# Moving a transposed activation tile by 128 bytes within SBUF in a two-layer float32 trunk

## The chip, the cores and the metric

The kernel runs on one core of a Trainium2 chip. The metric is the device time of one execution in microseconds (us), lower is better; the number given for a kernel is the median of several executions. One further execution of the kernel before was recorded by the hardware profiler, and all rows below come from that one.

## The reference

The input is one sequence of 256 tokens with 1024 channels in float32. Two layers follow each other, and each is a macaron: a feed-forward block, a token mixer, a second feed-forward block, each with an RMS norm before and after.

```python
def swiglu_ffn(x, w_in, w_out):
    gate, up = jnp.split(x @ w_in, 2, axis=-1)
    return (jax.nn.silu(gate) * up) @ w_out

for layer in range(DEPTH):
    g = norm_gains[layer]
    h = swiglu_ffn(rms_norm(x, g[0]), ffn_w_in[layer, 0], ffn_w_out[layer, 0])
    x = x + 0.5 * rms_norm(h, g[1])
    hn = rms_norm(x, g[2])
    # even layer: causal Conformer convolution; odd layer: HGRN2 gated recurrence
    x = x + rms_norm(m, g[3])
    h = swiglu_ffn(rms_norm(x, g[4]), ffn_w_in[layer, 1], ffn_w_out[layer, 1])
    x = x + 0.5 * rms_norm(h, g[5])
```

The hidden width of a feed-forward block (FFN) is 2816. Nearly all the arithmetic is matrix products of the activations with weights that are read from HBM once.

## The kernel before

**Precision.** Every float32 operand is split in two float32r tiles, a rounded high part and the remainder, and a product is made of three matmuls: high by high, high by low, low by high. `weight` (L121) fetches half a megabyte of weights into a `raw` tile (four buffers) and `split` (L135) makes `wh` on ScalarE (L136) and `wl` on VectorE (L137), ten buffers each.

**The transposed input.** `xt` (L101) holds the current activations transposed, channels on the partitions, as eight channel blocks `k` of 2048 bytes per partition: 256 columns of the high part, then 256 of the low part. `pre_norm` (L168) and the convolution's `turn` (L540) refill it ahead of each block. It is used in two ways:

- as the moving operand, with a weight block loaded into TensorE: `channels` (L324) in the FFNs. For each of two parts (PSUM tiles `mm` and `tr`) it runs eight matmuls of 512 columns on `wh` (L331) and then eight of 256 columns on `wl` (L333). `channel_pair` (L341) does the like with 256 columns throughout (L350 to L352), in the HGRN2 mixer;
- as the loaded (stationary) operand, with weights moving, 512 columns each: `project` (L291, L292, L295), and `mm3` (L140 to L142) from `boot` and from the convolution's output product.

The FFN's second product, `down` (L420), and the HGRN2 mixer's output product go through the same `mm3`, lines and weight tiles, but load other tiles: `b4` buffers (`b` in the profile) or `hid`.

An FFN loops over eleven chunks `c` of 256 hidden channels. For every chunk but the first it runs `up_both` twice (two calls of `channels`, b = 0 and 1, each with a part on `mm` and a part on `tr`), and then `down` for both halves of the tokens, 24 matmuls of 512 columns in a row.

**Where tiles stand.** Tiles of the pool `const` are placed one behind the other in the order of the code. Two tiles that nothing reads, `before_xt` and `after_xt`, stand around `xt`; together they take 512 bytes per partition. In the built program `xt` begins at byte 26144 of each partition, 32 beyond a multiple of 512. All buffers of `raw`, `wh`, `wl`, `b4`, `hid`, `e`, `ga` begin 160 beyond one. Slices of `xt`, of the weights and of `b4` that matmuls use are multiples of 512 bytes from the beginning of their tile, so a matmul on `xt` has its two operands 128 bytes apart modulo 512, and a matmul of `down` has them at the same place.

The order of the instructions on each engine is the order of the code; weights are fetched ahead, as far as buffers are free.

Of the kernel before, what the change touches and what calls it, by code (L numbers as in the profile page):

```python
# [8 lines left out]
F32 = mybir.dt.float32  # L9
# [7 lines left out]
P = 128  # L17
# [23 lines left out]
def trunk_kernel(  # L41
# [17 lines left out]
    const = ctx.enter_context(tc.tile_pool(name="const", bufs=1))  # L59
# [37 lines left out]
    pool.memset(ones, 1.0)  # L97

    xs = [const.tile([P, D], F32, name=f"x{t}") for t in range(NT)]
    const.tile([P, 88], F32, name="before_xt")  # L100
    xt_all = const.tile([P, NT * 2 * D], F32R, name="xt")  # L101
    const.tile([P, 40], F32, name="after_xt")
    xhl = xt_all.rearrange("p (k s t m) -> p k s t m", t=NT, s=2, m=P)
    gcol = const.tile([P, G_END], F32, name="gcol")

# [837 lines left out]
```

## Time and profile before

| | us |
|---|---|
| median of three runs | 1014.41 |
| lowest, highest | 1013.71, 1016.5 |
| the profiled execution | 1014.49 |
| its span, first to last instruction | 1012.6 |
| TensorE (PE) busy in it | 997.6 |
| VectorE (DVE) busy | 750.1 |
| ScalarE (ACT) busy | 548.2 |

The profile lists every instruction with its start and its length. On TensorE a matmul's length says little: matmuls are pipelined, each row shows some 390 ns for 512 columns, and the next one starts long before that has passed. What counts is the distance from one start to the next, called the pitch below. It is read from the timeline: the difference of two start times, divided by the number of matmuls between. Times in these rows are rounded to 10 ns, so a pitch is taken over many matmuls.

### The profile page before, as it was taken

To read this page: it belongs to the slowest core of one execution; us is meant where nothing else is said; L and a number is where in the kernel's file an instruction comes from. 1 tells how busy PE (TensorE), PEld (TensorE's weight loads), DVE (VectorE), ACT (ScalarE), POOL (GpSimd) and SP (SyncE) were. 2 spreads that over 40 slices of the span, in tenths; PEclk is the share of its full clock that TensorE was granted. 3 is DMA by queue.
4 is the path that set the end of the run, shared out by engine and by line. 5 is a ranking of instruction groups with operands and counts; after the bars stand their busy time and mean duration, and the time that the engine had idled before them with its cause. 6 is when DMAs were issued, how large, how long until landed. Compare 5 with 4: busy or idle time off the path is not lost.

```text
span 1012.6 us, 14787 instructions
## 1 busy us (share of the span) xinstructions
PE 997.6 (99%) x5412; PEld 853.8 (84%) x5412; DVE 750.1 (74%) x1274; ACT 548.2 (54%) x1000; POOL 56.3 (6%) x93
## 2 busy tenths in 40 slices
PE   9999999999899999999999999999999999999997
PEld 7888888878678888888888888889998888888886
DVE  6887667899888676767776767687788586767673
ACT  7656545764486555455755555584143384555542
POOL 1000000020021000000200000030001120000000
PEclk9999999999899999999999999999999999999999
DMA  7885645642527464646465646465232555555541
GB/s 250 277 286 166 213 170 178 236 176 97 178 102 241 166 209 167 224 155 222 167 198 176 210 165 221 163 210 181 81 125 92 179 192 183 180 195 192 184 146 41
DMA packets 50952, 182.06 MB, mean 180 GB/s; under 512 B 6048, under 2 KB 6176, under 8 KB 50880
## 3 DMA queue, kind: packets, MB, share of 16 engines
q1 hardware_dynamic: 50736, 181.09, 52.7%
q8 instruction: 42, 0.69, 0.3%
q14 instruction: 30, 0.25, 0.1%
q10 hardware_dynamic: 144, 0.03, 0.0%
HBM read 180.06 MB, written 1.05 MB: 179 GB/s over the span
## 4 chain that ended last, share of the span: by engine, by line
PE 91%; ACT 2%; DVE 2%; DMA 2%; POOL 1%; issue 1%; POOLq 0%; DVEq 0%; SPq 0%; ACTq 0%
PE mm L331 15%; PE tr L331 15%; PE acc L141 9%; PE acc L142 9%; PE acc L140 9%; PE mm L333 8%; PE tr L333 7%; PE mm L295 3%; PE mm L291 3%; PE mm L292 3%; PE tr L654 2%; DMA raw<-wts 2%; PE mm L351 2%; PE mm L352 2%; PE mm L350 1%; DVE wl L137 1%
## 5 line engine op out<-in xcount | busy, mean ns | idle before, releaser
L137 DVE TENSOR_TENSOR wl<-raw,wh 128x1024 fp32r<-128x1024 f32 (+1 forms) x386 | 400.1, 1059 | 88.1 <-ACT wh L136 62.8
L136 ACT CAST wh<-raw 128x1024 fp32r<-128x1024 f32 (+1 forms) x386 | 340.5, 921 | 125.2 <-DMA raw<-wts 74.9
L331 PE MATMUL mm<-xt,wh 128*128 128x512 f32 x640 | 164.1, 397 | 0.5 <-ACT wh L136 0.5
L331 PE MATMUL tr<-xt,wh 128*128 128x512 f32 x640 | 162.1, 395 | 0.0
L331 PEld LDWEIGHTS mm<-xt,wh 128*128 128x128 f32 x640 | 116.7, 188 | 25.7 <-ACT wh L136 1.3
L140 PE MATMUL acc<-wh,b 128*128 128x512 f32 x352 | 137.6, 391 | 0.0
L142 PE MATMUL acc<-wh,b 128*128 128x512 f32 x352 | 137.3, 390 | 0.0
L141 PE MATMUL acc<-wl,b 128*128 128x512 f32 x352 | 137.3, 390 | 0.0
L331 PEld LDWEIGHTS tr<-xt,wh 128*128 128x128 f32 x640 | 114.9, 188 | 20.9
L333 PEld LDWEIGHTS mm<-xt,wl 128*128 128x128 f32 x640 | 87.4, 188 | 7.4 <-DVE wl L137 0.2
L333 PEld LDWEIGHTS tr<-xt,wl 128*128 128x128 f32 x640 | 87.0, 188 | 7.4
L333 PE MATMUL mm<-xt,wl 128*128 128x256 f32 x640 | 90.0, 282 | 0.0
L333 PE MATMUL tr<-xt,wl 128*128 128x256 f32 x640 | 88.6, 281 | 0.0
L136 ACT CAST b<-e 128x256 fp32r<-128x256 f32 x80 | 32.5, 406 | 96.5 <-DVE e L412 96.5
L336 ACT COPY e<-tr 128x256 f32<-128x256 f32 x80 | 29.4, 367 | 89.6 <-PE tr L333 89.6
L142 PEld LDWEIGHTS acc<-wh,b 128*128 128x128 f32 x352 | 66.1, 188 | 13.9
L337 DVE TENSOR_TENSOR ga<-tr,e 128x256 f32<-128x256 f32 x80 | 33.7, 421 | 59.0 <-ACT e L336 58.8
L140 PEld LDWEIGHTS acc<-wh,b 128*128 128x128 f32 x352 | 66.1, 188 | 12.4
L141 PEld LDWEIGHTS acc<-wl,b 128*128 128x128 f32 x352 | 66.1, 188 | 12.4
L291 PE MATMUL mm<-wh,xt 128*128 128x512 f32 x176 | 70.7, 402 | 0.0
L292 PE MATMUL mm<-wl,xt 128*128 128x512 f32 x176 | 69.8, 397 | 0.0
L336 ACT COPY e<-mm 128x256 f32<-128x256 f32 x80 | 29.7, 371 | 51.4 <-PE mm L333 51.2
(180 smaller groups left out, 1253.6 us busy)
## 6 DMA issues: line engine op xcount, KB each, us to landing
raw<-wts SPq DMA_DIRECT2D x328, 512.0 KB, 4.8
b<-rows SPq DMA_DIRECT2D x10, 512.0 KB, 6.9
b<-x_turned SPq DMA_DIRECT2D x4, 256.0 KB, 6.1
x<-x_in SPq DMA_DIRECT2D x2, 512.0 KB, 7.6
out_dram<-x SPq DMA_DIRECT2D x4, 256.0 KB, 2.0
b<-dft SPq DMA_DIRECT2D x1, 371.0 KB, 6.4
ca<-masks SPq DMA_DIRECT2D x1, 192.0 KB, 4.6
b<-w_dw SPq DMA_DIRECT2D x1, 128.0 KB, 6.5
```

Source lines behind the costliest of these rows:

```text
L136: act.copy(dst_h, src)
L137: dve.tensor_tensor(dst_l, src, dst_h.bitcast(F32), op=ALU.subtract)
L140: pe.matmul(o, lh, rh, start=first, stop=False)
L141: pe.matmul(o, lh, rl, start=False, stop=False)
L142: pe.matmul(o, ll, rh, start=False, stop=last)
L291: pe.matmul(o, hi[:, k], wh[:, sl], start=k == 0, stop=False)
L292: pe.matmul(o, hi[:, k], wl[:, sl], start=False, stop=False)
L295: pe.matmul(o, a, w, start=False, stop=h == 1 and n == 3)
L331: pe.matmul(pair, block(ws[k // 2][0], k), xhl[:, k], start=k == 0, stop=False)
L333: pe.matmul(pair[:, 0], block(ws[k // 2][1], k), xhl[:, k, 0], start=False, stop=k == KD - 1)
L336: act.copy(cross, o[:, SEQ:])
L337: dve.tensor_tensor(res[:, part * SEQ : (part + 1) * SEQ], o[:, :SEQ], cross, op=ALU.add)
```

## The change

Padding is moved from behind `xt` to ahead of it. The sum stays 512 bytes, so nothing else moves.

```diff
     xs = [const.tile([P, D], F32, name=f"x{t}") for t in range(NT)]
-    const.tile([P, 88], F32, name="before_xt")
+    const.tile([P, 120], F32, name="before_xt")
     xt_all = const.tile([P, NT * 2 * D], F32R, name="xt")
-    const.tile([P, 40], F32, name="after_xt")
+    const.tile([P, 8], F32, name="after_xt")
```

`xt` now begins at byte 26272, 160 beyond a multiple of 512, as the weights do. Every instruction of all five engines stays, in the same order; in the built programs `xt`'s address is the only one that differs.

## Rows read from the trace of the kernel before

**Rows 1.** The page: TensorE's busy time and its granted clock in 40 slices.

```profile
PE 997.6 (99%) x5412; PEld 853.8 (84%) x5412; DVE 750.1 (74%) x1274; ACT 548.2 (54%) x1000; POOL 56.3 (6%) x93
...
PEclk9999999999899999999999999999999999999999
```

**Rows 2.** The page: the chain that ended last, by engine.

```profile
PE 91%; ACT 2%; DVE 2%; DMA 2%; POOL 1%; issue 1%; POOLq 0%; DVEq 0%; SPq 0%; ACTq 0%
```

**Rows 3.** Waits of PE: who for whom, us in total, times, longest.

```profile
PE mm L331 <- ACT wh L136: 0.5, 1, 0.5
```

**Rows 4.** Timeline of PE in an FFN chunk: start us, length us, instruction.

```profile
94.18 2.03 PE L331 MATMUL mm<-xt,wh 128*128 128x512 f32 x8
96.05 1.12 PE L333 MATMUL mm<-xt,wl 128*128 128x256 f32 x8
97.00 2.02 PE L331 MATMUL tr<-xt,wh 128*128 128x512 f32 x8
98.86 1.10 PE L333 MATMUL tr<-xt,wl 128*128 128x256 f32 x8
99.80 0.39 PE L140 MATMUL acc<-wh,b 128*128 128x512 f32 x1
...
100.72 0.39 PE L141 MATMUL acc<-wl,b 128*128 128x512 f32 x1
...
105.03 0.39 PE L142 MATMUL acc<-wh,b 128*128 128x512 f32 x1
```

**Rows 5.** Timeline of PE, convolution's output product: first and last of 28.

```profile
288.17 0.39 PE L142 MATMUL acc<-wh,xt 128*128 128x512 f32 x1
...
294.44 0.39 PE L142 MATMUL acc<-wh,xt 128*128 128x512 f32 x1
```

**Rows 6.** Timeline of PE, HGRN2 output product: 10 from 803.18, 28 from 805.50.

```profile
803.18 0.40 PE L141 MATMUL acc<-wl,b 128*128 128x512 f32 x1
...
805.27 0.39 PE L141 MATMUL acc<-wl,b 128*128 128x512 f32 x1
805.50 0.39 PE L142 MATMUL acc<-wh,b 128*128 128x512 f32 x1
...
811.62 0.39 PE L142 MATMUL acc<-wh,b 128*128 128x512 f32 x1
```

**Rows 7.** Timeline of PE, `channel_pair`, 256 columns: first and last of 61.

```profile
681.36 0.28 PE L350 MATMUL mm<-xt,wh 128*128 128x256 f32 x1
...
688.48 0.28 PE L350 MATMUL mm<-xt,wh 128*128 128x256 f32 x1
```

**Rows 8.** Timeline of PE, `channel_pair` later: first and last of 40.

```profile
737.02 0.29 PE L350 MATMUL mm<-xt,wh 128*128 128x256 f32 x1
...
741.70 0.28 PE L350 MATMUL mm<-xt,wh 128*128 128x256 f32 x1
```

**Rows 9.** Timeline of PE, `project`: first and last of 13.

```profile
301.90 0.40 PE L291 MATMUL mm<-wh,xt 128*128 128x512 f32 x1
...
304.70 0.40 PE L291 MATMUL mm<-wh,xt 128*128 128x512 f32 x1
```

**Rows 10.** Groups by line and shape: instructions, times, busy us, mean ns.

```profile
L331 PE MATMUL mm<-xt,wh 128*128 128x512 f32 x640 | 164.1, 397 | 0.5 <-ACT wh L136 0.5
...
L333 PE MATMUL mm<-xt,wl 128*128 128x256 f32 x640 | 90.0, 282 | 0.0
...
L291 PE MATMUL mm<-wh,xt 128*128 128x512 f32 x176 | 70.7, 402 | 0.0
...
L351 PE MATMUL mm<-xt,wh 128*128 128x256 f32 x128 | 36.4, 285 | 0.0
```

**Rows 11.** Windows of all engines, then of PE: busy us, clock, DMA share, GB/s.

```profile
0.00:12.00 12.00, 10.11 (x44) 8.57 (x45) 5.40 (x11) 7.86 (x16) 0.88 (x8) 1.00 0.82 271
...
350.00:366.70 16.70, 16.70 (x90) 1.00 0.58 189
```

**Rows 12.** Timeline of all engines: TensorE's weight load held by VectorE's split.

```profile
40.92 0.30 PEld L333 LDWEIGHTS mm<-xt,wl 128*128 128x128 f32 x2 [0.21 <-DVE wl L137]
```

## The prediction

> **What bounds the kernel now.** I read the page first. TensorE is busy for 997.6 of 1012.6 us at the full granted clock [rows 1], and it makes up 91% of the chain that ended last [rows 2]. Its waits on the makers of the weights are below a microsecond [rows 3]. So the time is a sum of matmul pitches, and the question is what sets a pitch. I read that from the timeline, start to start.
>
> In an FFN chunk eight L331 matmuls of 512 columns take 96.05 - 94.18 = 1.87 us, that is 233.8 ns each, and the next eight 1.86 us. Eight L333 matmuls of 256 columns take 0.95 and 0.94 us, some 118 ns each. `down` behind them needs 105.03 - 100.72 = 4.31 us for 19 matmuls of 512 columns, 226.8 ns each [rows 4]. `down` is about 3% quicker per matmul than L331, with the same number of columns and the same clock. It differs in many ways: another line, another order, other tiles.
>
> A cleaner pair stands in the two output products. They run the same lines L140 to L142 on the same weight buffers, and only the loaded tile differs. With `xt` loaded (128 bytes off the weights modulo 512) 27 steps take 294.44 - 288.17 = 6.27 us, 232.2 ns each [rows 5]. With `b4` loaded (the same place modulo 512) 27 steps take 811.62 - 805.50 = 6.12 us, 226.7 ns each [rows 6]. So 5.5 ns per matmul go with the place, and this is the row on which I build.
>
> Two more things are in these rows. The quick pitch isn't there from the start: after an interruption `b4`'s stream first runs 9 steps in 2.09 us, 232.2 ns each, and only then falls to 226.7 and stays [rows 6]. I call this the lead-in. And 256 columns at different places run at 118.7 ns (60 steps in 7.12 us) [rows 7], but once at exactly 120.0 (39 steps in 4.68 us) [rows 8]. No row shows a matmul of 256 columns whose operands stand at the same place modulo 512, and that is the unknown of this case.
>
> **The change part by part.** No instruction, DMA or wait is added, removed or moved. Only `xt`'s address changes, by 128 bytes, so that every matmul on `xt` gets its operands to the same place modulo 512. ScalarE and VectorE write `xt` at an address that moved; I cost that at nothing, since both are idle for a quarter of the span or more [rows 1].
>
> *Matmuls of 512 columns.* From 232.2 to 226.7 ns, by rows 5 and 6. The bounds are no gain (the lead-in never ends, since eight L331 in a row are fewer than the nine matmuls of the lead-in) and the full 5.5 to 7 ns each.
>
> *Matmuls of 256 columns.* I bound them by the nearest rows: 120.0 ns [rows 8] is a loss of 1.3, and half of the quick 512-column pitch, 226.7 / 2 = 113.3, is a gain of 5.4. Which? Going from 256 to 512 columns at different places costs 232.2 - 118.7 = 113.5 ns. So the columns themselves cost 113.5 per 256, and a surcharge of 118.7 - 113.5 = 5.2 ns per matmul is left, whatever its length. At the same place 512 columns cost 226.7, which is twice 113.3: the columns alone, no surcharge. I take it that the surcharge goes for 256 columns too, and use 113.3. This is my choice, and the weakest step.
>
> *FFN, L331 and L333.* One call of `channels` (rows 4: 1.87 + 0.95 + 1.86 + 0.94) takes 5.62 us. After: 16 x 226.7 + 16 x 113.3 ns = 3.63 + 1.81 = 5.44. It saves 0.18 us. There are 640 / 8 = 80 calls [rows 10]. In the first some 42 us weights come at the last moment: DMA runs at 271 GB/s there, and a weight load of TensorE is still held by VectorE's split at 40.92 [rows 11, 12]. What TensorE saves there it waits for weights instead, so I leave out three calls: 77 x 0.18 = 13.9 us. Behind that the weights leave room: in a steady chunk DMA moves 189 GB/s where the first 12 us show 271 [rows 11], and 2% more speed asks for 193.
>
> *`project`.* 3 x 176 = 528 matmuls [rows 10], at 233.3 ns now (12 steps in 2.80 us) [rows 9]. In full it would be 528 x 5.5 ns = 2.9 us, but this stream is cut by transposes and by the mixers' other matmuls, and each cut brings a lead-in of up to nine. I take half, 1.5.
>
> *`channel_pair`.* 3 x 128 = 384 of 256 columns [rows 10], at 118.7. 384 x 5.4 = 2.1 us; half of them come in short pieces, so I take 1.5.
>
> *`mm3` on `xt`.* The convolution's output product has 8 x 2 x 2 x 3 = 96 matmuls, 0.5 us, of which I take 0.3. `boot`'s 48 wait for weights and save nothing.
>
> *`down`.* Its lead-in behind L333 falls away if all streams keep one rhythm: 99.80 to 100.72 is 4 steps at 230 ns [rows 4], some 15 ns per chunk, and up to 9 x 5.5 = 50. For 40 chunks 0.6 to 2 us; I take 0.8.
>
> The sum is 13.9 + 1.5 + 1.5 + 0.3 + 0.8 = 18.0 us. The profiled execution took 1014.49 us, which is the median of the runs within 0.1. Forecast: 1014.5 - 18.0 = 996.5 us. Nothing is late next: the next limit is again TensorE's own pitch.
>
> **The rivals.**
>
> *Only part of it.* 256 columns stay at 118 to 120 ns, and each run of them throws the 512-column stream out of its quick rhythm. For: the 120.0 row exceeds 113.3 by a whole 6.7 ns and is as steady as the quick 226.7, so a steady rhythm for 256 columns may well be the long one. Against: the surcharge comes out alike for both lengths. Price: with a lead-in of 4 matmuls (rows 4) or 9 (rows 6) at each turn from 256 to 512 columns, eight L331 save between 8 x 6 - 15 = 30 ns and nothing. 77 calls x 2 parts x 0 to 30 ns = 0 to 4.6 us; `project` and `mm3` bring 1.8 as above; no lead-in goes from `down`. With 120 and all in one rhythm a call takes 3.63 + 1.92 = 5.55 us, which saves 0.07 x 77 = 5.4, plus 1.8. So 1.8 to 7.2 us, or 1007.3 to 1012.7; middle 1009.
>
> *Nothing at all.* The place isn't the cause, and rows 5 and 6 differ by something else that goes with the tile, such as its distance in memory from the weights or who wrote it. For: only one offset is seen for `xt`, so the trace can't tell "the same place modulo 512" from "`b4` rather than `xt`". Against: same lines, same shapes, same weights, and `hid` and `b4` agree in `down`. Price: 1014.5. The Trainium skill speaks for this rival and against the change: its page "TensorE: Matmul & The Clock Gate", section "Step-by-step: what each phase is for", says that TensorE has two independent read ports, so that loading the next weights takes no read bandwidth from the running matmul. By that rule the place of one operand to the other could not matter and the time would stay at 1014.5; rows 5 and 6, with 232.2 against 226.7 ns, speak against it here.
>
> *Slower.* The new place puts the streams of `xt` into the slowest steady rhythms that any row shows: 233.3 ns for 512 columns [rows 9] and 120.0 for 256 [rows 8]. That is one mechanism, a stream caught in a bad rhythm, in the 160 parts of the FFNs. A part takes 8 x 233.3 + 8 x 120.0 = 2.83 us against 5.62 / 2 = 2.81 now: 2 ns per matmul more on average gives 154 x 0.017 = 2.6 us; `project` is at 233.3 already in places and gives at most 0.6, `channel_pair` 384 x 1.3 = 0.5. Sum 3.7 us, 1018.2. It decides from the point where eight L331 and eight L333 together need over 2.83 us. Against it: at the same place, rows 4 and 6 show no 512-column stream that doesn't settle at 226.7.
>
> **How the numbers follow.** Forecast (both lengths gain) 0.50, only part 0.30, nothing 0.13, slower 0.07. The predicted time is that of the likeliest, 996.5. Its own range: if all lead-ins vanish, `project`, `channel_pair` and `mm3` bring their other 2.2 us, and `down` 1.2 more, so 993; if 256 columns get only half of their gain, 1280 x 2.7 ns = 3.5 us are missing, so 1000. The range that holds 8 in 10 reaches over the partial case as well: 993 to 1011. A measurement of this kernel can tell about 0.3%, 3 us, from no change. Faster by more: the forecast and nearly all of the partial case, 0.77. Within: the rest of that and "nothing", 0.16. Slower: 0.07.
>
> **What the profile would show.** Right: a call of `channels` takes 5.44 us instead of 5.62, eight L331 1.81 and eight L333 0.91; the convolution's output product settles at 226.7 like the other one; `down` starts without a lead-in; no new wait of PE on ScalarE or VectorE after 50 us. The partial case: eight L333 still 0.94 to 0.96 us, and L331 begins each run of eight at 230 or more. Nothing: rows 5 again at 232. Wrong altogether would be a PE that waits for weights in the steady chunks, or L331 above 1.87 us.

## The result and the profile after

| | before | after |
|---|---|---|
| median, us (same chip, four runs each) | 1014.61 | 1009.73 |
| ratio after to before, 95% interval | | 0.9948 [0.9933, 0.9963] |
| the profiled execution, us | 1014.49 | 1008.88 |
| its span, us | 1012.6 | 1007.0 |
| TensorE busy in it, us | 997.6 | 992.5 |

The kernel became 4.9 us faster, not 18. The sign and the place are as predicted, but the size is that of the rival "only part of it" (1007.3 to 1012.7, middle 1009), not that of the forecast (996.5). The stated range of 993 to 1011 holds the measured time only because it reaches over that rival; the forecast's own range ended at 1000.

The page of the changed kernel: TensorE's busy time, its granted clock in 40 slices, the chain that ended last by engine.

```profile
PE 992.5 (99%) x5412; PEld 854.8 (85%) x5412; DVE 749.7 (74%) x1274; ACT 548.6 (54%) x1000; POOL 53.6 (5%) x93
...
PEclk9999999999899999999999999999999999999999
...
PE 94%; DVE 2%; ACT 1%; DMA 1%; POOL 1%; issue 0%; DVEq 0%; POOLq 0%; SPq 0%; ACTq 0%
```

They answer to [rows 1, 2]. TensorE is still nearly all of the time, at the same clock, and it needs 5.1 us less. Waits of PE on `wh` and `wl` in the FFNs, after:

```profile
PE mm L331 <- ACT wh L136: 0.5, 1, 0.5
...
PE mm L333 <- DVE wl L137: 0.2, 1, 0.2
```

The first is word for word [rows 3]. The second is new; it stands at 41 us, where the prediction had left out what TensorE saves. All waits of PE together are 8.0 us, and were 8.4 before, so hardly anything was turned into a wait. The difference lies in the pitch, the distance from one start to the next. The timeline of PE after, around the place of [rows 4] (start us, length us, instruction; the row at 95.40 is the sixth of the eight that begin at 94.24):

```profile
88.68 1.98 PE L331 MATMUL mm<-xt,wh 128*128 128x512 f32 x8
90.49 1.12 PE L333 MATMUL mm<-xt,wl 128*128 128x256 f32 x8
91.44 2.00 PE L331 MATMUL tr<-xt,wh 128*128 128x512 f32 x8
...
94.24 2.00 PE L331 MATMUL mm<-xt,wh 128*128 128x512 f32 x8
...
95.40 0.39 PE L331 MATMUL mm<-xt,wh 128*128 128x512 f32 x1
...
96.08 1.11 PE L333 MATMUL mm<-xt,wl 128*128 128x256 f32 x8
97.03 2.00 PE L331 MATMUL tr<-xt,wh 128*128 128x512 f32 x8
...
99.82 0.40 PE L140 MATMUL acc<-wh,b 128*128 128x512 f32 x1
...
100.98 0.39 PE L142 MATMUL acc<-wh,b 128*128 128x512 f32 x1
...
105.06 0.39 PE L142 MATMUL acc<-wh,b 128*128 128x512 f32 x1
```

Four readings:

- Behind `down` (88.68 to 90.49) eight L331 take 1.81 us, 226.3 ns each within the rounding: the quick pitch from the first matmul on. That is what the prediction wanted everywhere.
- Behind a run of L333 it isn't so. From 94.24, five steps take 1.16 us (232 ns each) and only the last three, 95.40 to 96.08, run at 226.7. Eight together take 1.84 us instead of 1.87.
- Eight L333 take 0.95 us (90.49 to 91.44; 96.08 to 97.03), which is what they took before. Their single steps are 113, 119 and then six times 120.0 ns.
- `down` has a lead-in as well: 99.82 to 100.98 is 5 steps at 232 ns, and the next 18, up to 105.06, run at 226.7.

A part of `channels` (eight L331 and eight L333) so takes 2.793 us after (91.44 to 94.24: 2.80 with rounding), where the forecast had 2.72.

The uncut streams of 512 columns with `xt` did what was expected. The convolution's output product after, 26 steps, answers to [rows 5]:

```profile
286.81 0.39 PE L140 MATMUL acc<-wh,xt 128*128 128x512 f32 x1
...
292.70 0.39 PE L142 MATMUL acc<-wh,xt 128*128 128x512 f32 x1
```

5.89 us / 26 = 226.5 ns, against 232.2. `project` after, 12 steps, answers to [rows 9]:

```profile
301.51 0.39 PE L291 MATMUL mm<-wh,xt 128*128 128x512 f32 x1
...
304.23 0.39 PE L291 MATMUL mm<-wh,xt 128*128 128x512 f32 x1
```

2.72 / 12 = 226.7 ns, against 233.3. And `channel_pair`, 60 steps of 256 columns, answers to [rows 7]:

```profile
681.35 0.28 PE L350 MATMUL mm<-xt,wh 128*128 128x256 f32 x1
...
688.55 0.28 PE L350 MATMUL mm<-xt,wh 128*128 128x256 f32 x1
```

7.20 / 60 = 120.0 ns, against 118.7. So at the same place 512 columns become quicker and 256 columns become slower. 120.0 is the number of [rows 8], which the prediction kept as its bad end, although that row was measured at the old distance.

### The profile page after: what moved, and what is told of

Read it like the earlier page. It is cut to its first block, busy times and chain, and to the rows that moved or that the text cites. A ratio compares the mean times of both kernels' runs of the same rounds, so it can differ in the third digit from the quotient of the medians.

```text
span 1007.0 us, 14787 instructions
## 1 busy us (share of the span) xinstructions
PE 992.5 (99%) x5412; PEld 854.8 (85%) x5412; DVE 749.7 (74%) x1274; ACT 548.6 (54%) x1000; POOL 53.6 (5%) x93
## 4 chain that ended last, share of the span: by engine, by line
PE 94%; DVE 2%; ACT 1%; DMA 1%; POOL 1%; issue 0%; DVEq 0%; POOLq 0%; SPq 0%; ACTq 0%
PE tr L331 14%; PE mm L331 14%; PE acc L141 9%; PE acc L140 9%; PE acc L142 9%; PE tr L333 7%; PE mm L333 7%; PE mm L291 4%; PE mm L292 4%; PE mm L295 4%; PE tr L654 2%; PE mm L351 2%; PE mm L352 2%; PE mm L350 2%; DMA raw<-wts 1%; PE tr L175 1%
## 5 line engine op out<-in xcount | busy, mean ns | idle before, releaser
L331 PE MATMUL mm<-xt,wh 128*128 128x512 f32 x640 | 161.6, 393 | 0.5 <-ACT wh L136 0.5
L331 PE MATMUL tr<-xt,wh 128*128 128x512 f32 x640 | 160.7, 392 | 0.0
L331 PEld LDWEIGHTS mm<-xt,wh 128*128 128x128 f32 x640 | 116.9, 188 | 24.1 <-ACT wh L136 1.3
L331 PEld LDWEIGHTS tr<-xt,wh 128*128 128x128 f32 x640 | 115.0, 189 | 20.7
L333 PEld LDWEIGHTS mm<-xt,wl 128*128 128x128 f32 x640 | 87.5, 190 | 6.7 <-DVE wl L137 0.4
L333 PEld LDWEIGHTS tr<-xt,wl 128*128 128x128 f32 x640 | 87.3, 190 | 6.2
L333 PE MATMUL mm<-xt,wl 128*128 128x256 f32 x640 | 90.0, 282 | 0.2 <-DVE wl L137 0.2
L333 PE MATMUL tr<-xt,wl 128*128 128x256 f32 x640 | 89.2, 282 | 0.0
L337 DVE TENSOR_TENSOR ga<-tr,e 128x256 f32<-128x256 f32 x80 | 33.7, 421 | 55.6 <-ACT e L336 55.6
```

The source lines that it names most:

```text
L331: pe.matmul(pair, block(ws[k // 2][0], k), xhl[:, k], start=k == 0, stop=False)
L333: pe.matmul(pair[:, 0], block(ws[k // 2][1], k), xhl[:, k, 0], start=False, stop=k == KD - 1)
L337: dve.tensor_tensor(res[:, part * SEQ : (part + 1) * SEQ], o[:, :SEQ], cross, op=ALU.add)
```

## The experiments

In all tables the pitch of a line is the mean over all its matmuls, from the start times in the trace of one execution, those before a wait or an interruption left out. The distance is the place of the moving operand less that of the loaded one, in bytes. In the FFN `xt` moves, so before has -128 and after 0; in `project`, where `xt` is loaded, the sign is the other way.

### e1: the pitch by itself

The model is left out. There are only matmuls, each with its own weight load, in 58 streams of one shape and 42 matmuls each, cut by four transposes; loaded and moving slices stand at chosen places. One execution was recorded, at a granted clock of 1.00.

```python
CASES = [(a, a, n) for a in (0, 32, 64, 96) for n in (512, 256, 384, 240, 128)]
CASES += [(160, (160 + d) % 512, n) for d in range(32, 512, 32) for n in (512, 256)]
CASES += [(s, 160, n) for s in (32, 288, 128, 192) for n in (512, 256)]
```

> This kernel leaves out the model: it copies its input to the output and runs, on one pair of tiles and with nothing else on the chip, 58 streams of 42 float32r matmuls, each stream with its own place of the loaded and the moving operand modulo 512 bytes and its own number of columns. Four 128-column transposes stand between two streams. It measures the disputed cost by itself: the steady pitch, start to start. Theory A (what stays per matmul is a constant): at equal places the steady pitch is the time of N columns at 2.4 GHz plus 13.3 ns, whatever the absolute place, so 226.7 ns for 512 columns, 120.0 for 256, 173.3 for 384, 113.3 for 240. Theory B (blocks): the steady pitch is 13.3 ns for each block of 128 bytes that the moving operand touches, so 226.7 and 120.0 at a place 32 beyond a multiple of 128 (17 and 9 blocks) but 213.3 and 106.7 at a multiple of 128 (16 and 8), and 106.7 for 240 columns at 32. Theory C (my prediction's choice: columns alone): 256 columns settle at 113.3 in some of the equal places. For unequal places all three expect 512 columns at some 232 ns on average at a distance of 128 bytes either way; whether other distances are as bad, none of them says.

Measured, the timeline of PE: of each stream the 24 matmuls tagged `flow`, and the one behind them.

```profile
46.50 5.60 PE L49 MATMUL flow<-moving,loaded 128*128 128x512 f32 x24
51.94 0.62 PE L49 MATMUL tail<-moving,loaded 128*128 128x512 f32 x2
...
54.74 3.04 PE L49 MATMUL flow<-moving,loaded 128*128 128x256 f32 x24
57.62 0.40 PE L49 MATMUL tail<-moving,loaded 128*128 128x256 f32 x2
...
106.33 2.84 PE L49 MATMUL flow<-moving,loaded 128*128 128x128 f32 x24
109.01 0.39 PE L49 MATMUL tail<-moving,loaded 128*128 128x128 f32 x2
...
224.93 5.76 PE L49 MATMUL flow<-moving,loaded 128*128 128x512 f32 x24
230.53 0.62 PE L49 MATMUL tail<-moving,loaded 128*128 128x512 f32 x2
...
233.25 2.88 PE L49 MATMUL flow<-moving,loaded 128*128 128x256 f32 x24
235.97 0.40 PE L49 MATMUL tail<-moving,loaded 128*128 128x256 f32 x2
```

The first two pairs have distance 0: 5.44 us / 24 = 226.7 ns for 512 columns and 2.88 / 24 = 120.0 for 256. The last two have distance 192: 5.60 / 24 = 233.3 and 2.72 / 24 = 113.3. The pair between is 128 columns at distance 0: 2.68 / 24 = 111.7, hardly less than 256 columns cost. All distances (steady pitch, ns, from the 24 steps):

```
distance    0 (256)   32 (288)  64 (320)  96 (352)  128 (384)  160 (416)  192 (448)  224 (480)
512 columns  226.7     233.3     228.9     233.3     232.1      234.2      233.3      233.3
256 columns  120.0     116.7     117.75    120.0     118.7      118.5      113.3      118.3
```

The numbers in brackets ran as those beside them: the pattern repeats after 256 bytes, not 512. The absolute place does nothing: both operands at 0, 32, 64 or 96 give the same (one stream, the very first, had 227.5). At distance 0 384 columns took 173.3, so from 256 to 384 and from 384 to 512 columns the pitch grows by 53.3 ns, that is 2.4 columns per ns. At that rate 512, 384 and 256 columns cost 213.3, 160.0 and 106.7, and each of the three has 13.3 ns on top, as theory A has it; B (blocks of 128 bytes) and C (113.3 at the same place) fail. Only 240 columns took 112.0 where A had 113.3, near the 111.7 of 128 columns. So at the same place the surcharge doesn't vanish, it becomes the same for 256 columns and more. At 128, where before stood, it is 18.8 for 512 columns and 12.0 for 256. The change trades one for the other. One stream at distance 128, with the loaded operand moved instead, ran at 233.3 instead of 232.1, as in [rows 9]: a distance can have more than one steady rhythm.

### e2: the kernel's own mixtures at all places

The same, with streams as they stand in the kernel, for 64 pairs of distances: u to `wh` (512 columns) and v to `wl` (256 columns). The cut is shortened, and its comments are added here.

```python
run(bank("lead"), [high] * 8 + [rest] * 8)       # four times, channels
run(bank("flow", 1), [high, rest] * 16)          # by turns
run(bank("tail", 1), [hi, lo, hi] * 8)           # mm3
```

> Leaves out the model: it copies its input to the output and runs streams of float32r matmuls alone. Where the first of these kernels ran one length and one pair of places at a time, this one runs the kernel's own mixtures: eight matmuls of 512 columns and eight of 256 in turns (as `channels` does), 512 and 256 alternating, and high-low-high with 512 columns (as mm3 does), for all 64 pairs of distances u and v, modulo 256 bytes, of the moving operand behind the two loaded ones (in the last mixture the transposed input is the loaded one). Theory A (each length has its own rhythm for its own distance, and turning from one length to the other costs a lead-in): at u = v = 0, the places of the changed kernel, a turn of 16 takes 8 x 226.7 + 8 x 120.0 = 2.773 us plus some 0.02 of lead-in; at u = v = 128, before, some 2.805; at u = 0, v = 192 the steady part would be 8 x 226.7 + 8 x 113.3 = 2.720 us. Theory B (the two lengths share one rhythm, so a good distance of one doesn't help beside a bad one of the other): 2.80 wherever u and v differ.

Measured, some of the table (us for eight of each length, "8 and then 8" as the mean of the second and third part; ns per matmul for mm3, the mean of steps 10 to 21):

```
u, v              0, 0    128, 128   192, 192   64, 64   0, 192   64, 0
8 and then 8      2.793    2.808      2.773     2.763    2.780    2.787
by turns          2.831    2.806      2.827     2.825    2.773    2.720
mm3, xt loaded    226.7    232.5      228.9     233.3    231.0    234.5
```

(0, 0) and (128, 128) are after and before. 2.793 is to the nanosecond what most parts of after show. 2.808 is the mean of two unequal parts, 2.817 and 2.799, as before's own parts alternate between 2.799 and 2.821. At (64, 64) the two were 2.784 and 2.741, and `mm3` at (0, 192) doesn't settle: its last 18 steps have 232.2. The pair to look at is (0, 192). Its two lengths by themselves run at 226.7 and 113.3, so 8 of each would be 2.72; together they take 2.780. And (64, 0) by turns takes 2.720, though by themselves its two run at 228.9 and 120.0. The timeline of PE of both: first matmuls of two parts at (0, 192), and of two rounds of eight turns at (64, 0).

```profile
156.84 0.39 PE L49 MATMUL lead<-moving,loaded 128*128 128x512 f32 x1
...
159.62 0.39 PE L49 MATMUL lead<-moving,loaded 128*128 128x512 f32 x1
...
402.03 0.39 PE L49 MATMUL flow<-moving,loaded 128*128 128x512 f32 x1
...
404.75 0.39 PE L49 MATMUL flow<-moving,loaded 128*128 128x512 f32 x1
```

2.78 and 2.72 us. The pitch doesn't belong to the matmul but to the stream: neighbours share a rhythm. Neither theory holds whole: A has (0, 0) right and (0, 192) wrong by 40 to 60 ns, and B's 2.80 for all unlike distances fails at (64, 0) by turns.

### e3, e4, e5 and e8: other places of xt in the kernel

The changed kernel with the padding split otherwise, everything else as it was: 56 and 72 elements in e3 (shown), 104 and 24 in e4, 8 and 120 in e5, 80 and 136 in e8. In e3 `xt` is 256 bytes beyond the weights, in e4 64 before them, in e5 64 beyond. In e8 all of them, weights and `b4` too, begin at a multiple of 512; `xt` there begins at byte 26112 (the 480 bytes in its expectation are a slip).

```diff
-    const.tile([P, 120], F32, name="before_xt")
+    const.tile([P, 56], F32, name="before_xt")
     xt_all = const.tile([P, NT * 2 * D], F32R, name="xt")
-    const.tile([P, 8], F32, name="after_xt")
+    const.tile([P, 72], F32, name="after_xt")
```

> The changed kernel with `xt` 256 bytes behind the weights modulo 512 instead of at the same place (padding 56 and 72). Theory modulo 512 (what the change's name says): not the same place, so a pitch like before, 1014 us. Theory modulo 256 (the first experiment's streams repeat after 256 bytes): the same pitches as after the change, 1009.7 us, ratio 0.995.

> `xt` 64 bytes ahead of the weights modulo 256 (padding 104 and 24). From the streams of the first experiment: 512 columns with `xt` moving at 233.3 ns, 256 columns at 113.3, with `xt` loaded 512 columns at 228.9. Theory A (each length its own rhythm): a call of `channels` takes 16 x 233.3 + 16 x 113.3 = 5.55 us or a little more, where before has 5.62 and after 5.59; `channel_pair` at 113.3 saves 384 x 5.4 = 2.1 us; `project` at 228.9 saves up to 528 x 3.6 = 1.9. Sum: 77 x 0.07 + 2 + 1 = 8 us, some 1006 us. Theory same place (only equal places gain): 1014 us.

> `xt` 64 bytes behind the weights modulo 256 (padding 8 and 120). From the streams of the first experiment: with `xt` moving 512 columns at 228.9 and 256 at 117.75, with `xt` loaded 512 at 233.3. Theory A: a call of `channels` takes 5.55 us or a little more, `channel_pair` saves 0.4 us, `project` loses up to 0.5: 1009 us. Theory same place: 1014 us.

> 80 and 136 elements of padding around xt: xt at 480 bytes modulo 512 less 0, that is everything behind it moves by 352 bytes, and xt, wh, wl and b4 all begin at a multiple of 512, where the changed kernel has all of them 160 beyond one. Only the distance matters: as the changed kernel, 1009 to 1011 us, L331 at 229.4 and L333 at 119.0 ns. The place by itself matters (a slice that begins at a multiple of 512 is read in fewer pieces): other pitches than these, by over 1 ns, and a time that is 3 us or more away.

| | xt less weights | us | ratio to before, 95% | L331 | L333 | project |
|---|---|---|---|---|---|---|
| before | -128 | 1014.6 to 1015.6 | | 232.5 | 118.6 | 232.3 to 233.5 |
| after | 0 | 1009.73 | 0.9948 [0.9933, 0.9963] | 229.4 | 119.1 | 228.4 to 229.3 |
| e3 | 256 | 1010.69 | 0.9953 [0.9938, 0.9968] | 229.5 | 119.0 | as after |
| e8 (one run) | 0, all at 0 | 1010.59 | | 229.5 | 119.1 | 228.3 to 229.3 |
| e4 | -64 | 1008.10 | 0.9932 [0.9916, 0.9949] | 232.9 | 114.3 | 229.7 to 230 |
| e5 | 64 | 1009.59 | 0.9941 [0.9926, 0.9956] | 229.7 | 116.8 | 233.0 to 233.8 |

e3 and e8 are after again, pitch by pitch: the 512 in "the same place modulo 512" is really 256, and only the distance counts. e8 in the timeline of PE, as after at 94.24:

```profile
94.44 2.00 PE L331 MATMUL mm<-xt,wh 128*128 128x512 f32 x8
96.28 1.12 PE L333 MATMUL mm<-xt,wl 128*128 128x256 f32 x8
97.23 2.00 PE L331 MATMUL tr<-xt,wh 128*128 128x512 f32 x8
```

Theory A has the direction of e4 and e5 right (1006 and 1009 us expected, 1008.1 and 1009.6 measured), and "only equal places gain", with 1014, fails. e4 gains as much as after, in the other length. The timeline of PE in e4:

```profile
93.70 2.02 PE L331 MATMUL mm<-xt,wh 128*128 128x512 f32 x8
95.56 1.07 PE L333 MATMUL mm<-xt,wl 128*128 128x256 f32 x8
96.47 2.02 PE L331 MATMUL tr<-xt,wh 128*128 128x512 f32 x8
```

Eight L331 take 1.86 us as in [rows 4], eight L333 0.91 us instead of 0.95. The sum of one steady step of each is 346.7 ns in e4 (233.3 + 113.3) and in after (226.7 + 120.0): what one length wins the other loses. e5 shows that it is the sign that counts, too: L331 is quicker than before there, and `project`, where the operands change roles and 64 becomes -64, is not.

### e6: each length at its own best distance

`wl` alone is moved by 64 bytes, so that L331 has distance 0 and L333 has -64. This is the test of the step that failed, since it offers both 226.7 and 113.3 to the kernel.

```diff
         hi = new(sb, [P, 1024], F32R, "wh", 10)
+        if stream[0] <= 1 and at < 1:
+            new(sb, [P, 16], F32, "before_wl", 1)
         lo = new(sb, [P, 1024], F32R, "wl", 10)
+        if stream[0] <= 1 and at < 1:
+            new(sb, [P, 112], F32, "after_wl", 1)
```

> The changed kernel with 64 bytes of padding ahead of the wl buffers (448 behind them): xt and wh at 160 modulo 512, wl at 224. L331 keeps the distance 0, L333 gets the distance -64 = 192 modulo 256, at which the streams by themselves ran 226.7 ns (512 columns) and 113.3 ns (256 columns). Theory A (the prediction's step with the missing price put right: each length keeps its own rhythm, whatever stands next to it): a part of channels takes 8 x 226.7 + 8 x 113.3 = 2.72 us instead of 2.794, 154 parts save 11.4 us; in down and project a third of the matmuls (wl moving) goes from 226.7 to 228.9, 592 x 2.2 ns = 1.3 us; 1009.7 - 11.4 + 1.3 = 999.6 us. Theory B (neighbours in one stream share one rhythm, so a pitch of one length can't be added to a pitch of the other): a part takes the 2.780 us that the mixed stream measured at this pair of distances, 154 x 0.013 = 2.0 us saved; down and project run their mixture at 231.0 instead of some 228, 1776 x 3 ns = 5.3 us lost; 1009.7 - 2.0 + 5.3 = 1013.0 us. L333's mean decides beside the time: 113.3 by A, 116 to 119 by B.

Measured: 1013.94 us, ratio 0.9990 [0.9981, 1.0000]. L333 (now L337) runs at 117.4, L331 (L335) at 230.0, `down` at 232.0. Theory B holds, theory A is out by 14 us. The timeline of PE in e6:

```profile
94.04 2.00 PE L335 MATMUL mm<-xt,wh 128*128 128x512 f32 x8
95.88 1.11 PE L337 MATMUL mm<-xt,wl 128*128 128x256 f32 x8
96.82 2.00 PE L335 MATMUL tr<-xt,wh 128*128 128x512 f32 x8
```

2.78 us for a part (94.04 to 96.82), as e2 had measured for (0, 192). `down` and the HGRN2 output product, whose `wl` is now 64 bytes off the loaded tile, lost 4 ns on each of their 1152 matmuls, some 4.7 us, the largest part of what separates e6 from the changed kernel.

### e7: the quickest mixture of e2

e6's padding, `xt` 64 bytes beyond `wh` and at the same place as `wl`, and L331 and L333 by turns.

```diff
             for k in range(KD):
                 pe.matmul(pair, block(ws[k // 2][0], k), xhl[:, k], start=k == 0, stop=False)
-            for k in range(KD):
                 pe.matmul(pair[:, 0], block(ws[k // 2][1], k), xhl[:, k, 0],
                           start=False, stop=k == KD - 1)
```

> The kernel of e6 with xt at 224 (8 and 120 elements of padding), so that xt stands 64 behind wh and at the same place as wl, and with L331 and L333 taken in turn, block by block, in channels (512 columns on wh, 256 on wl, next block). In the mixed streams this pair and this order were the quickest of all, 2.720 us for a part. Theory B (one rhythm per stream, and the table of mixed streams carries over to the kernel): 154 parts save 154 x (2.794 - 2.720) = 11.4 us against the changed kernel; down runs at 231.0 instead of 227.8, 1152 x 3.2 ns = 3.7 us lost; project and mm3 on xt at 234.5 instead of 228.7, 624 x 5.8 = 3.6 us lost; channel_pair within 0.5. 1009.7 - 11.4 + 7.3 = 1005.6 us, and L331 and L333 together start 340 ns apart. Theory A (each length its own rhythm): 8 x 228.9 + 8 x 120.0 = 2.79 us for a part, nothing saved, 1009.7 + 1.3 + 1 = 1012 us. A table that doesn't carry over at all would show a part of 2.77 to 2.83 us and a time of 1013 or more.

Measured: 1010.83 us, ratio 0.9954 [0.9939, 0.9969], 5 us above what theory B gave. The timeline of PE says why. First matmuls of two parts in one chunk, and of two parts in the next:

```profile
59.13 0.39 PE L335 MATMUL tr<-xt,wh 128*128 128x512 f32 x1
...
61.85 0.39 PE L335 MATMUL mm<-xt,wh 128*128 128x512 f32 x1
...
75.65 0.40 PE L335 MATMUL tr<-xt,wh 128*128 128x512 f32 x1
...
78.45 0.40 PE L335 MATMUL mm<-xt,wh 128*128 128x512 f32 x1
```

The first part takes 2.72 us, the second 2.80, the same instructions at the same places. The steps are 226.7 and 113.3 by turns in the one, 232.5 and 117.5 in the other, each repeated to within a nanosecond. In the long stretches of the trace a chunk keeps one rhythm for all its four parts, and the next chunk has the other. Of 160 parts 66 are quick (up to 2.76), 79 slow (2.79 to 2.80), the other 15 are longer, cut by a wait or by other work. 79 x 0.08 = 6.3 us, a little more than the 5 that are missing. (`down` at 231.8 cost 0.9 more than theory B has, `project` at 230.9 instead of 234.5 cost 1.9 less.) So the 2.720 of e2 does come in the kernel, but one stream has two steady rhythms, and e2 had shown only one.

### e11 and e12: what chooses the rhythm

e7 with one exchange each among the matmuls around the turn from `down` to `channels`. e11: the first part of a chunk begins with two L331 and two L333. e12: in the last step of `down` the matmul on `wl` comes last.

```diff
 (e11)
+            turns = [(k, s) for k in range(KD) for s in range(2)]
+            if part == 0 and cols_[0] == 0:
+                turns[1:3] = [(1, 0), (0, 1)]
...
 (e12)
         pe.matmul(o, lh, rh, start=first, stop=False)
+        if turn:
+            pe.matmul(o, ll, rh, start=False, stop=False)
...
+            turn = (k, n) == (n_k - 1, 1) and n_k == 2 and not last
```

> The kernel of e7 with one exchange: in the first part of each chunk, the one behind down, the first two L331 stand next to each other and then the first two L333, and from there on the two take turns as before. In e7 the alternating stream ran in two steady rhythms, 2.720 and 2.800 us for a part, and kept the one that it fell into behind down up to the end of the chunk, one chunk the quick one, the next the slow one. Theory: which one it is hangs on the first matmuls behind down, so this exchange changes the pattern of chunks: all quick 1010.8 - 80 x 0.08 = 1004.5 us, all slow 1017, or turn by turn again 1010.8. Rival: the rhythm is set by something outside TensorE (weights arriving, buffers): the pattern of e7 stays as it was, chunk by chunk, 1010.8 us.

> The kernel of e7 with another exchange: in the last step of down the matmul on wl comes last instead of second, so that the stream enters the next chunk from another step. Same theory and rival as for e11: 1004.5 us if every chunk falls into the quick rhythm, 1017 if every one falls into the slow one, 1010.8 if they take turns as in e7.

Measured: e11 1005.57 us, ratio 0.9901 [0.9888, 0.9915]; e12 1004.60 us, ratio 0.9895 [0.9881, 0.9908]. 140 and 138 of the 160 parts are quick now, 3 and 6 slow. The timeline of PE in e12, first matmuls of three parts in the chunk that was slow in e7:

```profile
74.73 0.39 PE L339 MATMUL tr<-xt,wh 128*128 128x512 f32 x1
...
77.45 0.39 PE L339 MATMUL mm<-xt,wh 128*128 128x512 f32 x1
...
80.17 0.39 PE L339 MATMUL tr<-xt,wh 128*128 128x512 f32 x1
```

2.72 us each. The pattern of chunks changed with the order of a few matmuls, so the rhythm hangs on how the stream is entered; the rival, by which weights or buffers set it and the pattern stays, fails. e12 has a check of this in itself: in four chunks six small matmuls (`tr<-b,b`) stand between `down` and `channels`, so that its exchange isn't next to the entry. There quick and slow chunks take turns as in e7, and all 6 slow parts stand there. First matmuls of two parts in each of the first two of these chunks, e12:

```profile
108.78 0.40 PE L339 MATMUL tr<-xt,wh 128*128 128x512 f32 x1
...
111.58 0.40 PE L339 MATMUL mm<-xt,wh 128*128 128x512 f32 x1
...
126.55 0.39 PE L339 MATMUL tr<-xt,wh 128*128 128x512 f32 x1
...
129.27 0.39 PE L339 MATMUL mm<-xt,wh 128*128 128x512 f32 x1
```

2.80 and 2.72 us. Why either exchange leads to the quick rhythm isn't known, nor what makes e7's chunks take turns. Both were tried because they alter the entry, and they could as well have led to the slow one.

### e9 and e10: the changed kernel beside its neighbour

The changed kernel and the kernel of e4, once more, on the chip of e11 and e12.

> The changed kernel once more, unaltered, beside the next three, so that they can be compared on one chip: 1009 to 1010.5 us, a ratio of 0.995 to before, L331 at 229.4 and L333 at 119.0 ns.

> The kernel of e4 (xt 64 bytes before the place of the weights modulo 256) once more, beside the changed kernel. By the parts measured so far a call of channels takes 2 x 2.773 us against 2 x 2.794, 80 x 0.042 = 3.3 us less; channel_pair 384 x 5.2 ns = 2.0 us less; project and mm3 on xt 624 x 1.0 ns = 0.6 us more: 4.7 us less by the sum, 1.6 us less as measured in e4. It beats the changed kernel if the intervals of the two ratios lie apart: 1006 to 1008.5 us expected, ratio 0.992 to 0.9935. If the two intervals overlap, the two are the same by these runs.

Measured: 1009.08 us, ratio 0.9944 [0.9931, 0.9956], and 1008.38 us, ratio 0.9928 [0.9914, 0.9941]. The intervals overlap, so these two are the same by these runs. That of e12 lies below both, that of e11 below the changed kernel's and against e10's (0.9915 and 0.9914). With 1004.6 us, e12 beats before by 10.7 us and the changed kernel by 4.5.

e4 and e10 are one program, and they show that the order of the instructions alone doesn't fix the rhythm. The first stream of `channel_pair` (192 matmuls of 256 columns at distance -64), 60 steps in e4 and then in e10:

```profile
679.43 0.28 PE L350 MATMUL mm<-xt,wh 128*128 128x256 f32 x1
...
686.23 0.28 PE L350 MATMUL mm<-xt,wh 128*128 128x256 f32 x1
```

```profile
680.15 0.28 PE L350 MATMUL mm<-xt,wh 128*128 128x256 f32 x1
...
687.22 0.28 PE L350 MATMUL mm<-xt,wh 128*128 128x256 f32 x1
```

6.80 / 60 = 113.3 ns in the one execution, 7.07 / 60 = 117.8 in the other, from the first steps to the last of the stream, 0.8 us in all. The traces don't say what differed at its entry. So a pitch of the tables above is that of one execution, and what e11 and e12 gain rests on the medians of four.

## Why the prediction was wrong in size

**What held.** The cause is the distance of the two operands, and nothing else that goes with the tile: e3 to e5 move `xt` alone and the pitches follow. "Nothing at all" fell with that. The prediction had set a page beside this rival: the Trainium skill's "TensorE: Matmul & The Clock Gate", section "Step-by-step: what each phase is for", says that loading the next weights takes no read bandwidth from the running matmul. By that the distance could not matter, and e1 measured 226.7 and 233.3 ns for the same matmul at two distances; the measurement decides. Why the distance matters stays open: every matmul here had its own weight load, and no run took the loads away. That 512 columns on `xt` would go from 232.2 to 226.7 was right wherever a stream is long enough: `project`, the convolution's output product, L331 behind `down`. No new wait appeared but one of 0.2 us.

**The step that failed: 113.3 ns for 256 columns at the same place.** It was the prediction's own choice, "the columns alone, no surcharge". It came from one subtraction, 232.2 - 118.7 at distance 128, which takes for granted that the surcharge is the same for both lengths. There it is not: by e1 256 columns alone cost 106.7, not 113.5, and the surcharge is 18.8 ns for 512 columns and 12.0 for 256. It is the same for both at distance 0, where it is 13.3, so 256 columns cost 120.0. L333 was to save 86 ns in a call of `channels` (16 x 5.4) and lost 8 (16 x 0.5). `channel_pair` was to save 1.5 us and lost 0.4.

**The second part of the same term: all 16 L331 at 226.7.** The prediction dropped the lead-in, since all streams would have one rhythm. 256 and 512 columns don't share one, so each turn from L333 to L331 costs five steps at 232 ns. Only the parts right behind `down` escape. The mean of L331 went from 232.5 to 229.4 where 226.7 was forecast.

**The sum with what was measured.** L331: 1280 x 3.1 = 4.0 us. L333: 1280 x -0.5 = -0.6. So `channels` brought 3.3 us, where the prediction had 13.9. `project` 2.1 (predicted 1.5), `mm3` on `xt` 0.5 (0.3), `channel_pair` -0.4 (1.5), `down` -0.2 (0.8, and its lead-in stayed). Together 5.4 us, against 5.6 between the two profiled executions and 4.9 between the medians. The prediction's smaller terms are off by 2 us at most each; `channels` alone by 10.6.

**The rivals.** "Only part of it" named both mechanisms, 120.0 as the steady rhythm of 256 columns and a lead-in at each turn, and its bounds for eight L331 (nothing to 30 ns) hold the measured 25. (Its sum has a slip: 8 x 6 - 15 is 33, not 30.) It deserved the larger chance by its own evidence: 120.0 to the hundredth over 39 steps [rows 8] was a row, 113.3 was not one. That the row's 120.0 is also the pitch after is luck as far as the runs go: it belongs to distance -128, where the same line ran at 118.7 as well [rows 7], and e1 has 118.7 there. "Slower" did not come, as no `xt` stream of 512 columns became slower than before. (Its "2 ns per matmul" should be 1: 0.017 us on 16.)

**What the experiments add.** The 2.72 us of the forecast do exist for a part of `channels`, but not through two good pitches put side by side (e6: 2.780). They came from a mixture, measured as a mixture (e2) and entered rightly (e11, e12). Even that doesn't make up the forecast: `down` and `project` pay for the moved `wl`. With `wl` 64 bytes beyond `wh`, as here, e2 has no place of the loaded tile at which `mm3` runs below 231.0 ns; with `wl` 64 bytes before `wh` it has 228.9 at (64, 128), which no kernel tried.

## What to carry to other kernels

On a kernel that is bound by TensorE, read the pitch of each stream from start to start, and take a price from a stream of the same length and the same neighbours. A pitch of another length, halved or doubled, was wrong here by 6.7 ns in 113. Where padding is to be tuned, measure the mixture that the kernel really issues for all distances in one small kernel, then look in the kernel's own trace whether it runs in the quick or the slow rhythm; a steady pitch in one chunk and another in the next is a sign that the entry chooses. Look at more than one execution: the same program ran one stream at 113.3 ns in e4 and at 117.8 in e10.

## What the runs showed of the hardware

- The steady pitch of a stream of float32r matmuls, each with its own weight load, hangs on the distance between moving and loaded operand, modulo 256 bytes: 226.7 to 234.2 ns for 512 columns, 113.3 to 120.0 for 256 (e1). The absolute place did nothing in e1 and e8.
- The best distance for one length is among the worst for the other (0: 226.7 and 120.0; 192: 233.3 and 113.3).
- Below 256 columns little is left to win: 128 columns took 111.7 ns at distance 0 (e1).
- A stream can have two steady rhythms with the same instructions and places, 2.720 and 2.800 us for 16 matmuls, and keeps the one that it is in through a whole chunk (e7). Exchanging two matmuls at its entry changed which (e11, e12).
- The same program can run a stream in either rhythm: 256 columns at distance -64 went at 113.3 ns in e4 and at 117.8 in e10.
